# A three-part reordering in a Strassen-tiled flow-matching layer: the late half of pair 0, the first weight splits, and the last raw loads

## The chip, the cores and the metric

The kernel runs on one core of one Trainium2 chip. The metric is device time of one execution in microseconds (us). One core has TensorE (PE, matrix products into PSUM), VectorE (DVE), ScalarE (ACT), GpSimd (POOL), SyncE (SP, which here issues most DMAs) and 16 DMA engines. Each engine works through its own queue of instructions in order.

## The reference

One layer (`DEPTH = 1`) of a flow-matching backbone on 1024 sample tokens and 128 prompt tokens, `D_MODEL = 1024`, all in float32. For each group of tokens:

```python
h = rmsnorm(x, norm1_g) * (1.0 + scale1) + shift1
z = h @ w_in
# u_s5, u_f, g_s5, g_f are slices of z
y_s5, finals = s5_branch(u_s5, h0, p)        # two scans over a state space, GLU
y_f = fourier_branch(u_f)                    # 2D FFT, real part
m = sigmoid(g_s5) * (y_s5 @ w_proj_s5) + sigmoid(g_f) * (y_f @ w_proj_fft)
x = x + gate1 * (m @ w_out)
h2 = rmsnorm(x, norm2_g) * (1.0 + scale2) + shift2
ff = (silu(h2 @ w_ffn_gate) * (h2 @ w_ffn_up)) @ w_ffn_down     # D_FF = 2816
x = x + gate2 * ff
y = rmsnorm(x, final_norm_g)
```

The outputs are y of both groups and the final scan states of the prompt. The change works in the line of `ff`: the gate and up products and the down projection.

## The kernel before

All products are made in a split form: an operand is written as a high part (a cast to the `fp32r` type, on ACT) and a low part (operand minus high part, on DVE or POOL), and PE makes three products of the parts. So each weight block costs one cast and one subtraction, called a split here, before PE can use it.

**Feed-forward stage.** The 2816 hidden columns are 22 tiles of 128, taken as 11 pairs (`p` = 0 to 10). `ffn_unit(p, kind, which)` makes the gate (`"g"`) or up (`"u"`) half of a pair. It uses a Strassen-Winograd scheme: from the two weight tiles `w0` and `w1` four blocks `a11`, `a12`, `a21`, `a22` are taken, three sums and one more are formed on POOL, seven blocks are split, and seven products are made, in PSUM banks Z, W, X, Y, Z, X, Y. `which` says for which tokens: `"A"` is token tiles 0 to 4, `"B"` is token tiles 5 to 8, `"AB"` is both. The operands of B (`TB`) are written while the first unit already runs. So pair 0 runs in two halves: the early half `ffn_unit(0, ..., "A")` first, and the late half `ffn_unit(0, ..., "B")` after pair 2 in the kernel before. For the late half the splits are on DVE (function `le`), for the AB units on POOL.

The weights come through a ring of three buffers `ws`, with one exception: the gate weights of the late half (name `g0B`) go into the tile `gb` of the pool `pgb`, which is one buffer. The same buffer holds, one after the other, the gate rows `gb2`, the copy `hb` of token tile 6 in the first unit, and then `ra{m}`, the finished hidden rows of pair `m`, read back from the DRAM tensor `ffd` by `ra_load(m)`.

While pair `p` runs, the side work `a_steps(p - 1)` combines `ra` of the pair before in DVE sums, splits the results into `stg` (cast on ACT, subtraction on DVE) and writes them to the DRAM tensor `ad`: these are the Strassen operands of the down projection. It is hooked between the products of the units; pair 1 has no side work, and pair 0's is done under pair 10.

**Down stage.** The pairs are grouped in blocks: `BLK = [[0], [1, 2], [3, 4], [5, 6], [7, 8]]`, and `STD = [9, 10]`, which is made without Strassen. `prep(m, ki)` forms the weight block for product key `ki` (sums on POOL, or DVE for pairs 1 and 2), loads the activation operand A from `ad` (`load_at`) and splits the weight block (`split2`: cast on ACT, subtraction on POOL for pair 0, on DVE otherwise). The A operands of a block use a ring of 10 buffers; a block of two pairs has 14. The first block's sums go into ACC by copies on ACT (L1465), all others by additions on DVE (L1467). The seventh weight block of pair 0 takes a buffer `ftA` that the last unit of the feed-forward stage still uses.

For `STD`, `load_a(m)` reads the raw hidden rows `fr` from `ffd` and `prep_std` splits them on POOL; `gate_x` multiplies the sums by gate2 (DVE) and adds x1 (POOL), which `x1_load` reads into the ring `fr` (six buffers with the raw rows) or, one time in four, into `xr` (two buffers). At the end come the norm and the stores.

What sets the order: a planner simulates the engines and puts every instruction into its engine's queue as soon as, in its model, its operands and buffers are ready; where several are ready, the one earlier in the program goes first. So a load whose buffer is free can be queued far ahead of its place in the program. `tc.issue_after(ins)` holds a block's instructions behind `ins` on the same queue: in `load_a` and `x1_load`, behind `last["A"]`, and in the up units behind the last `ra_load`. No wait is added by it.

Of the kernel before, what the change touches and what calls it, by code (L numbers as in the profile page):

```python
# [61 lines left out]
def tile_flow_step(ctx: ExitStack, tc: tile.TileContext, a, o):  # L62
    nc = tc.nc
    V, S, PL, PE, SY = nc.vector, nc.scalar, nc.gpsimd, nc.tensor, nc.sync
# [23 lines left out]
    def f32(ap):  # L88
        return ap.bitcast(F32)
# [38 lines left out]
    mods, last = {}, {}  # L128
# [558 lines left out]
    def prep(q):  # L687
        return s5_prep2(q, *s5_prep(q))

    pre, run_ = [prep(0)], []  # L690
    gate(ORD[0])
    pre.append(prep(1))
    run_.append(s5_run(0, pre[0][1]))
    for q in range(NB):
        if q < NB - 1:
            run_.append(s5_run(q + 1, pre[q + 1][1]))
        if q:
            gate(ORD[q])
        if q == NB - 1:
            for p in ORD[NB:]:  # L700
                gate(p)
        s5_out(q, pre[q][0], pre[q][2], *run_[q])
        if q < NB - 2:
            pre.append(prep(q + 2))
# [416 lines left out]
    BLK = [[0]] + [[m, m + 1] for m in range(1, 9, 2)]  # L1121
    STD = [9, 10]

    def ra_load(m):
        ra[m] = pgb.tile([128, 2, NS], F32, tag="gb", name=f"ra{m}")
        for f in range(2):
            i_ = SY.dma_start(out=ra[m][:, f], in_=ffd[2 * m + f][:, 0:NS]).ins
        ra_ins[:] = [i_]

    def ffn_unit(p, kind, which, hooks=()):  # L1130
# [90 lines left out]
        if not gate_:  # L1221
            for s in which:
                _, nt, c0 = subs[s]
                st_ = dict(out=ffd[2 * p:2 * p + 2, :, c0:c0 + 128 * nt].rearrange("f p c -> p f c"),
                           in_=fsl[s].rearrange("p f t e c -> p f (t e c)"))
                if p == NF // 2 - 1:
                    last_st.append(st_)
                else:
                    SY.dma_start(**st_)
            if len(which) == 2 and p < STD[0] and p != 2:  # L1230
                ra_load(p)

    ps1 = open_pool("psF1", space=PSUM)
# [39 lines left out]
    def take(n, h=None):  # L1273
# [7 lines left out]
        return go  # L1281

    ffn_unit(0, "g", "A", [take(1), take(1), take(0), take(0), take(0, hk[0]), take(1, hk[1]), take(1, hk[2])])
    ffn_unit(0, "u", "A", [take(1, hk[3]), take(1), take(2, hk[4]), take(1, hk[5]), take(0), take(1), take(0)])
    pst_.release()
    ps2 = open_pool("psF2", space=PSUM)
    open_sub("B", {z: ps2 for z in "ZWXY"}, pm0, "m0a")
    ad = {m: dram.tile([7, 128, 2, 512], F32, tag=f"ad{m}", name=f"ad{m}") for m in range(STD[0])}
# [3 lines left out]
    def a_steps(m):  # L1292
        a_ = {f"{f}{z}": ra[m][:, f, h] for f in range(2) for z, h in (("L", LO), ("H", HI))}

        def comb(out, x, y, op=ALU.subtract):
            V.tensor_tensor(a_[out], a_[x], a_[y], op)  # L1296

        def p6():
            comb("0H", "0H", "1H", ALU.add)
            comb("0L", "0H", "0L")  # L1300

        def one(ki):
            nonlocal nstg
            src = a_[dict(P1="0L", P2="1L", P6="0L", P7="0L", P4="1H", P5="0H", P3="1L")[KEYS[ki]]]
            st_ = stg[:, nstg % 3]
            nstg += 1
            S.copy(out=st_[:, 0], in_=src)  # L1307
            V.tensor_tensor(st_[:, 1], src, f32(st_[:, 0]), ALU.subtract)  # L1308
            if m or ki not in (2, 3, 4):
                S.dma_start(out=ad[m][ki], in_=f32(st_))  # L1310

        def do(*fs):
            return lambda: [one(f) if isinstance(f, int) else f() for f in fs]

        p7a, p7b = (lambda: comb("1L", "1L", "0L")), (lambda: comb("0L", "1H", "0L"))
        st = [do(0), do(1), do(5), p6, do(p7a, 6), do(2), do(3), do(p7b, 4)]
        return [no] * 6 + st if m else [no] * 3 + st + [no] * 3

    for p in range(1, NF // 2):
        hk = a_steps((p - 1) % STD[0]) if p > 1 else [no] * 14  # L1320
        ffn_unit(p, "g", "AB", hk[:7])
        ffn_unit(p, "u", "AB", hk[7:])
        if p == 2:
            ffn_unit(0, "g", "B")
            ffn_unit(0, "u", "B")
            ra_load(2)
        if p == NF // 2 - 2:
            ra_load(0)

# [13 lines left out]
    AT, BT, PT, raws, araw, wraw = {}, {}, {}, {}, {}, {}  # L1343
# [12 lines left out]
    def a_new(name):  # L1356
        return pA.tile([128, 2, 512], F32R, tag="A", bufs=NA, name=name)

    def b_new(name):
        return ringed("b", [128, 2, 512], F32R, "wh", NWH, "R", NR, name)  # L1360

    def split2(w, src, eng=None):
        S.copy(out=w[:, 0], in_=src)
        (eng or V).tensor_tensor(w[:, 1], src, f32(w[:, 0]), ALU.subtract)  # L1364
        return w

    def load_at(m, ki):
        key = KEYS[ki]
        if (m, key) in AT:
            return  # L1370
        if m == 0 and ki in kept:
            AT[m, key] = kept[ki]
            return
        AT[m, key] = A1[:, ki] if m == 0 and ki < 2 else a_new(f"A{m}_{ki}")
        last["A"] = SY.dma_start(out=f32(AT[m, key]), in_=ad[m][ki]).ins

    def load_a(m):
        araw[m] = []
# [34 lines left out]
    def sub(out, x, y, op=ALU.subtract, eng=None):  # L1413
        (eng or PL).tensor_tensor(out, x, y, op)  # L1414

    def prep(m, ki):
        key = KEYS[ki]
        w0L, w0H, w1L, w1H = raws[m]
        if key == "P6":
            sub(w0H, w1H, w0H, eng=V if m in VSUB else PL)  # L1420
            sub(w0L, w0H, w0L, ALU.add, V if m in VSUB else PL)
        if key == "P5":
            sub(w1L, w1L, w0L)
            sub(w0L, w1H, w0L)
        bsrc = dict(P1=w0L, P2=w1L, P6=w0L, P7=w0H, P4=w1L, P5=w0L, P3=w1H)[key]
        if m == 0:
            B = wr.tile([128, 2, 512], F32R, tag="wh" if ki < 6 else "ftA", bufs=NWH if ki < 6 else 1, name=f"B0{key}")
        else:
            B = b_new(f"B{m}{key}")
        load_at(m, ki)  # L1430
        BT[m, key] = split2(B, bsrc, PL if m == 0 else V)

    def prep_std(m, ki):
        w0L, w0H, w1L, w1H = raws[m][0:4]
# [229 lines left out]
    for ki in range(2):  # L1664
        for m in BLK[1]:
            load_at(m, ki)
# [124 lines left out]
```

## Time and profile before

| | |
|---|---|
| three timed runs | 1547.5, 1546.07, 1540.08 us; median 1546.07 |
| the profiled execution | 1545.5 us, span 1543.5 us |
| mean granted clock of PE | 0.976 of full speed |
| PE busy | 1466.8 us, 95% of the span, 8999 matmuls |
| DVE, POOL, ACT busy | 61%, 43%, 37% of the span |
| DMA | 243.84 MB, mean 158 GB/s |

Times in the profile are microseconds from the start of the span; the span is the profiled execution without what lies around it. A busy share is an average over stages. An idle time is written in brackets with what ended it. PE's clock is given as the share of full speed that was granted: 1.00 is 2.4 GHz, and 0.5 is the lower level, 1.2 GHz. The feed-forward stage begins at about 745 us and ends at 1263 us; the down stage lasts from there to the end.

### The profile page before, as it was taken

How to read it: one execution, taken by the hardware profiler on the slowest of the kernel's cores; microseconds unless marked ns; L12 is line 12 of the kernel's file. 1: busy time of each engine (PE TensorE's matmuls, PEld its weight loads, DVE VectorE, ACT ScalarE, POOL GpSimd, SP SyncE). 2: the span in 40 equal slices, each digit the busy share in tenths (PEclk: the TensorE clock that was granted, in tenths of full speed). 3: DMA queues.
4: the chain of work that ended last, by engine and by line, in shares of the span. 5: the costliest groups of instructions: out<-in, count | busy, mean ns of one | idle time of the engine just before them, and what ended most of it. 6: DMA issues, size and time to landing. Idle time of an engine off the chain costs nothing. (4 is left out here: it accounts for less than half of the span.)

```text
span 1543.5 us, 23975 instructions
## 1 busy us (share of the span) xinstructions
PE 1466.8 (95%) x8999; PEld 1316.9 (85%) x8999; DVE 938.4 (61%) x1838; ACT 567.0 (37%) x1096; POOL 663.4 (43%) x606
## 2 busy tenths in 40 slices
PE   6999999999999999989999799999999999999995
PEld 3899998899968778877689799999999988888774
DVE  5647989995264335379942445554345547666778
ACT  7423334343543122255542233433333434212223
POOL 4900000000132111355687478877777982231354
PEclk9999999999989999999999899999999999999998
DMA  9242233232526643454513425444445557565713
GB/s 327 100 138 88 81 107 113 80 104 93 173 65 205 202 145 110 150 205 164 191 59 113 181 96 199 158 183 162 173 168 209 207 206 285 206 232 203 260 57 123
DMA packets 101984, 243.84 MB, mean 158 GB/s; under 512 B 15710, under 2 KB 46047, under 8 KB 101868
## 3 DMA queue, kind: packets, MB, share of 16 engines
q1 hardware_dynamic: 93228, 210.84, 39.9%
q10 hardware_dynamic: 8640, 31.46, 5.2%
q8 instruction: 71, 1.16, 0.3%
q14 instruction: 45, 0.37, 0.1%
HBM read 172.51 MB, written 69.74 MB: 157 GB/s over the span
## 5 line engine op out<-in xcount | busy, mean ns | idle before, releaser
L94 POOL TENSOR_TENSOR wh_glu<-ws_glu,wh_glu 128x512 fp32r<-128x512 f32 x4 | 5.1, 1278 | 338.0 <-ACT wh_glu L93 338.0
L271 PE MATMUL g<-h,wh_g 128*128 128x384 f32 (+1 forms) x432 | 147.3, 341 | 0.0
L272 PE MATMUL g<-h,wh_g 128*128 128x384 f32 (+1 forms) x432 | 147.1, 341 | 0.0
L273 PE MATMUL g<-h,wh_g 128*128 128x384 f32 (+1 forms) x432 | 146.3, 339 | 0.0
L1308 DVE TENSOR_TENSOR stg<-ra,stg 128x512 fp32r<-128x512 f32 x63 | 69.4, 1112 | 72.2 <-ACT stg L1307 72.0
L1414 POOL TENSOR_TENSOR wd<-wd,wd 128x512 f32<-128x512 f32 x25 | 36.7, 1481 | 110.6 <-DMA wd<-in_w_d 38.3
L272 PEld LDWEIGHTS g<-h,wh_g 128*128 128x128 f32 x432 | 81.4, 188 | 0.2 <-issue 0.2
L271 PEld LDWEIGHTS g<-h,wh_g 128*128 128x128 f32 x432 | 81.2, 188 | 0.3 <-issue 0.3
L273 PEld LDWEIGHTS g<-h,wh_g 128*128 128x128 f32 x432 | 81.2, 188 | 0.2 <-issue 0.2
L94 POOL TENSOR_TENSOR wh_pj<-ws_pj,wh_pj 128x512 fp32r<-128x512 f32 x16 | 22.1, 1382 | 103.9 <-ACT wh_pj L93 93.4
L1467 DVE TENSOR_TENSOR acc<-acc,U 128x1024 f32<-128x1024 f32 x34 | 41.4, 1219 | 26.8 <-PE U L1448 26.6
L1307 ACT CAST stg<-ra 128x512 fp32r<-128x512 f32 x63 | 38.3, 617 | 44.7 <-DVE ra L1296 32.2
L963 DVE TENSOR_TENSOR wh_out<-ws_out,wh_out 128x512 fp32r<-128x512 f32 x32 | 33.8, 1071 | 24.6 <-ACT wh_out L962 24.6
L1448 PE MATMUL q<-B,A 128*128 128x512 f32 x192 | 45.7, 394 | 0.5 <-DVE acc L1467 0.3
L1448 PEld LDWEIGHTS q<-B,A 128*128 128x128 f32 x192 | 35.8, 187 | 9.5 <-DVE acc L1467 0.8
L1296 DVE TENSOR_TENSOR ra<-ra 128x512 f32<-128x512 f32 x36 | 43.5, 1209 | 0.3
L963 POOL TENSOR_TENSOR wh_out<-ws_out,wh_out 128x512 fp32r<-128x512 f32 x16 | 22.4, 1405 | 48.8 <-ACT wh_out L962 45.7
L923 DVE TENSOR_TENSOR sgc<-sgc,p 128x384 f32<-128x384 f32 x24 | 13.3, 554 | 48.4 <-PE p L106 48.4
L977 PE MATMUL o<-wh_out,m 128*128 128x512 f32 x96 | 37.1, 414 | 4.1 <-ACT scr0b L1059 4.1
L636 DVE TENSOR_TENSOR ta<-X,Sg 128x56 f32<-128x56 f32 (+10 forms) x88 | 39.1, 445 | 1.2
L639 DVE TENSOR_TENSOR X<-X,tb 128x56 f32<-128x56 f32 (+10 forms) x88 | 39.1, 452 | 0.9
L962 ACT CAST wh_out<-ws_out 128x512 fp32r<-128x512 f32 x48 | 28.3, 615 | 30.4 <-PE o L979 20.3
(1550 smaller groups left out, 4522.3 us busy)
## 6 DMA issues: line engine op xcount, KB each, us to landing
ad<-stg ACTq DMA_DIRECT2D x60, 512.0 KB, 2.8
A<-ad SPq DMA_DIRECT2D x60, 512.0 KB, 5.8
wa<-in_w_ada SPq DMA_DIRECT2D x48, 512.0 KB, 6.0
ws_out<-in_w_out SPq DMA_DIRECT2D x24, 512.0 KB, 4.0
wd<-in_w_d SPq DMA_DIRECT2D x22, 512.0 KB, 9.1
ind<-in SPq DMA_DIRECT2D x54, 192.0 KB, 1.9
ws_g<-in_w_in SPq DMA_DIRECT2D x18, 512.0 KB, 3.5
sgc<-ind SPq DMA_DIRECT2D x48, 192.0 KB, 3.6
```

Of the source, the lines that this page charges most:

```text
L271: PE.matmul(ps, w[:, 0, wsl], hi, start=first, stop=False)
L272: PE.matmul(ps, w[:, 0, wsl], lo, start=False, stop=False)
L273: PE.matmul(ps, w[:, 1, wsl], hi, start=False, stop=last)
L636: V.tensor_tensor(A, src, Sc[:, 0, lv, gs].unsqueeze(1).unsqueeze(3).to_broadcast(shp), ALU.mult)
L639: V.tensor_tensor(dst, dst, B[:, ::-1], ALU.add)
L963: (eng or PL).tensor_tensor(w[:, 1, :], src, f32(w[:, 0, :]), ALU.subtract)
L977: PE.matmul(p, mc[t][0][:, k, ts_], w[n][:, 0], start=(k == 0), stop=False)
L1296: V.tensor_tensor(a_[out], a_[x], a_[y], op)
L1307: S.copy(out=st_[:, 0], in_=src)
L1308: V.tensor_tensor(st_[:, 1], src, f32(st_[:, 0]), ALU.subtract)
L1448: PE.matmul(ps, A[:, va], B[:, vb], start=(first and ti == 0 and i == 0), stop=(last and ti == n - 1 and i == 2), skip_group_check=True)
L1467: V.tensor_tensor(dst, dst, ps, ALU.add)
```

## The change

The late half of pair 0 moves from behind pair 2 to behind pair 1. With it `ra_load(1)` moves behind the late half, and `ra_load(2)` follows pair 2 as for the later pairs. The weight splits of pair 0 in the down stage go from POOL to DVE. The raw loads of pairs 9 and 10, and the x1 loads, are held behind the last A load of block 5 and 6 in place of that of block 7 and 8.

```diff
@@ -1227,7 +1227,7 @@
                     last_st.append(st_)
                 else:
                     SY.dma_start(**st_)
-            if len(which) == 2 and p < STD[0] and p != 2:
+            if len(which) == 2 and 1 < p < STD[0]:
                 ra_load(p)
 
     ps1 = open_pool("psF1", space=PSUM)
@@ -1320,10 +1320,10 @@
         hk = a_steps((p - 1) % STD[0]) if p > 1 else [no] * 14
         ffn_unit(p, "g", "AB", hk[:7])
         ffn_unit(p, "u", "AB", hk[7:])
-        if p == 2:
+        if p == 1:
             ffn_unit(0, "g", "B")
             ffn_unit(0, "u", "B")
-            ra_load(2)
+            ra_load(1)
         if p == NF // 2 - 2:
             ra_load(0)
 
@@ -1372,7 +1372,9 @@
             AT[m, key] = kept[ki]
             return
         AT[m, key] = A1[:, ki] if m == 0 and ki < 2 else a_new(f"A{m}_{ki}")
-        last["A"] = SY.dma_start(out=f32(AT[m, key]), in_=ad[m][ki]).ins
+        i_ = SY.dma_start(out=f32(AT[m, key]), in_=ad[m][ki]).ins
+        if m <= BLK[-2][-1]:
+            last["A"] = i_
 
     def load_a(m):
         araw[m] = []
@@ -1428,7 +1430,7 @@
         else:
             B = b_new(f"B{m}{key}")
         load_at(m, ki)
-        BT[m, key] = split2(B, bsrc, PL if m == 0 else V)
+        BT[m, key] = split2(B, bsrc, V)
 
     def prep_std(m, ki):
         w0L, w0H, w1L, w1H = raws[m][0:4]
```

## Rows read from the trace of the kernel before

**Rows 1.** two stretches of 100 us: busy us, instructions; clock, DMA share, GB/s.

```profile
800.00:900.00 100.00, 90.80 (x666) 90.01 (x665) 38.21 (x68) 32.58 (x67) 60.72 (x51) 0.93 0.34 124
1200.00:1300.00 100.00, 96.04 (x612) 89.35 (x613) 56.40 (x78) 41.11 (x75) 70.14 (x55) 0.98 0.67 245
```

**Rows 2.** waits of PE: who, for whom, us, times, longest.

```profile
PE ZBg0B L1162 <- ACT wh_g0Ba L962: 5.5, 1, 5.5
```

**Rows 3.** timeline of PE: start us, us, operation, count, [idle before <- releaser].

```profile
871.24 1.56 PE L1162 MATMUL YBu2AB<-TB,wh_u2ABs 128*128 128x256 f32 x12
878.32 3.29 PE L1162 MATMUL ZBg0B<-TB,wh_g0Ba 128*128 128x256 f32 x12 [5.52 <-ACT wh_g0Ba L962]
...
892.33 1.58 PE L1162 MATMUL ZBg0B<-TB,wh_g0Ba 128*128 128x256 f32 x12
...
906.46 1.92 PE L1162 MATMUL ZAg3AB<-TA,wh_g3ABa 128*128 128x320 f32 x12
```

**Rows 4.** timeline of the SP queue around the late half of pair 0.

```profile
872.56 0.33 SPq L1138 DMA_DIRECT2D ws_g0B<-in_w_g  x1
...
900.01 0.33 SPq L957 DMA_DIRECT2D ws_g3AB<-in_w_g  x1
```

**Rows 5.** timeline of POOL: last reader of the buffer that g0B loads into.

```profile
763.09 1.28 POOL L1076 TENSOR_TENSOR TB<-hb,TB 128x512 fp32r<-128x512 f32 x1 [2.14 <-ACT TB L1074]
```

**Rows 6.** line 963, the splits: ns min/median/max, first and last start.

```profile
L963 DVE TENSOR_TENSOR wh_u0Ba<-ws_u0B,wh_u0Ba x3: 680/686/1742, 892.3 to 898.2; 128x512 fp32r<-128x512 f32 x3
```

**Rows 7.** one stretch of the late half, columns as in Rows 1.

```profile
892.00:906.50 14.50, 14.50 (x126) 14.50 (x125) 9.19 (x17) 5.64 (x12) 6.80 (x6) 1.00 0.42 146
```

**Rows 8.** the first 14 us of the down stage, columns as in Rows 1.

```profile
1263.50:1277.50 14.00, 10.35 (x39) 7.97 (x38) 2.78 (x3) 5.12 (x7) 10.92 (x11) 0.88 0.98 352
```

**Rows 9.** timeline of all engines where the down stage begins.

```profile
1263.54 2.97 PE L1448 MATMUL U<-B0P,A 128*128 128x512 f32 x12
...
1271.38 0.62 ACT L1363 CAST B0P<-wd 128x512 fp32r<-128x512 f32 x1 [3.16 <-POOL fsA L1190]
1271.90 1.92 ACT L1465 COPY acc<-U 128x1024 f32<-128x1024 f32 x2
...
1272.96 2.50 PE L1448 MATMUL U<-B0P,stg 128*128 128x512 f32 x6 [3.65 <-ACT acc L1465]
```

**Rows 10.** line 1364, splits of the down stage: ns min/median/max.

```profile
L1364 POOL TENSOR_TENSOR B0P<-wd,B0P x7: 1252/1292/1743, 1256.8 to 1273.2; 128x512 fp32r<-128x512 f32 x7
L1364 DVE TENSOR_TENSOR B1P<-wd,B1P x7: 680/685/1219, 1284.3 to 1320.5; 128x512 fp32r<-128x512 f32 x7
```

**Rows 11.** the SP queue in the last two blocks of the down stage.

```profile
1393.78 9.57 SPq L1375 DMA_DIRECT2D A<-ad  x3
...
1407.87 20.38 SPq L1375 DMA_DIRECT2D A<-ad  x10
...
1447.85 1.37 SPq L1382 DMA_DIRECT2D fr<-ffd  x3
```

**Rows 12.** timeline of POOL, first splits of the last pairs' activations.

```profile
1454.61 1.40 POOL L1364 TENSOR_TENSOR A<-fr,A 128x512 fp32r<-128x512 f32 x1 [23.00 <-DMA fr<-ffd]
```

**Rows 13.** timeline of DVE in the same place.

```profile
1457.61 3.48 DVE L1364 TENSOR_TENSOR B<-wd,B 128x512 fp32r<-128x512 f32 x2
```

**Rows 14.** timeline of PE in the same place.

```profile
1465.74 1.65 PE L1448 MATMUL V<-B7P,A 128*128 128x512 f32 x3 [2.50 <-DVE acc L1467]
...
1468.47 1.48 PE L1448 MATMUL V<-B7P,A 128*128 128x512 f32 x3
```

**Rows 15.** that stretch as a whole, columns as in Rows 1.

```profile
1461.00:1478.40 17.40, 14.20 (x49) 10.41 (x48) 12.97 (x10) 4.99 (x9) 9.90 (x7) 0.80 0.52 173
```

**Rows 16.** timeline of PE, first products of the last full block.

```profile
1416.66 0.86 PE L1448 MATMUL U<-B7P,A 128*128 128x512 f32 x3
...
1419.46 0.85 PE L1448 MATMUL Y<-B7P,A 128*128 128x512 f32 x3
```

**Rows 17.** DMA issues, 1400 to 1420 us: count, KB, us to landing.

```profile
A<-ad SPq DMA_DIRECT2D x8, 512.0 KB, 4.8
```

## Prediction

> **What bounds the kernel now.** I read the busy time by stretches of 100 us first. TensorE (PE) is the bound: in the down stage and in the feed-forward stage it is busy nearly all the time, so only the stretches where it falls short can pay. Two of them lie where the change works [rows 1]: 90.8 of 100 us at 800 to 900, and 96.0 at 1200 to 1300. A third, at 1461 to 1478, shows in a narrower cut [rows 15]. The table of PE's waits then names who ends each gap; the largest in the touched code is one of 5.5 us for the first split weight of the late gate unit, g0B [rows 2]. The timelines of PE, of SP's queue and of POOL tell why each gap is there. Outside these stretches PE runs through, so a gap that closes moves all later work forward, as long as DMA and VectorE (DVE) can follow.
>
> **Part 1: the late half behind pair 1.** The last product of pair 2 starts at 871.24, and pair 3 starts at 906.46 [rows 3]. A late product has 12 matmuls; ten of them run from 892.33 to 906.46, so one takes 1.41 us. Pair 2 therefore ends at 872.65, and 33.8 us pass for 14 late products that need 14 x 1.41 = 19.8 us: 14.0 us are lost, in gaps and at a lower clock behind them. The cause stands in SP's queue: the load of g0B's weights is issued only at 872.56 [rows 4], when pair 2 is over, because it goes into the one buffer `gb`, which then holds ra1, the input of the side work of pair 2. With the change, nothing is loaded into that buffer before the late half: its previous reader, the split of `hb`, is over at 764.4 [rows 5], long before pair 1 ends. The load can then lie under the early half and pair 1. The step takes all its instructions along: on SP the two loads into `gb`, u0B's two weight loads and one store, and behind them ra1's two loads, which pass from the end of pair 1 to the end of the late half; ra2's two no longer wait for the late half. ra1's sums and splits stay under pair 2, in the second half of their hooks, and as many as before.
>
> What could be late next: the seven splits of each late unit are on DVE. Uncontended one takes 0.69 us, at worst 1.74 [rows 6]. While u0B ran at full pace, DVE was busy 9.2 of 14.5 us with splits and sums together [rows 7], so it has 5.3 us in 14.5 to spare. Pair 2's second gate weight needs a slot that u0B's splits free. Before, the same load for pair 3 went out at 900.01, 6.5 us before pair 3, and PE did not wait for it [rows 3, 4]. So the gain is bounded by 14.0 above, and by nothing below if these covers fail. I take 13.5, near the upper end, since u0B already ran without a gap on the same engines.
>
> Here the Trainium skill speaks against the move (page "SBUF — State Buffer", section "Who interferes with whom"): a VectorE instruction with two SBUF inputs and a GpSimd instruction that reads SBUF block one another for a whole instruction. The trace agrees in that the same split takes 0.69 or 1.74 us.
>
> **Part 2: first weight splits on DVE.** The down stage begins at 1263.54, makes 36 matmuls' worth of work and stops: the next product waits 3.65 us, until 1272.96, for ACT's copy of U out of PSUM [rows 9]. That copy was ready long before, but on ACT it is queued behind a cast at 1271.38, which waits for POOL's last product of the feed-forward stage (fsA). POOL is late because seven splits of 1.29 us each, 9.0 us, stand among its work [rows 10]; it is busy 10.9 of 14.0 us [rows 8]. On DVE the same split takes 0.69 us (B1's row), 4.8 us in all, and DVE is busy only 2.8 of these 14.0 us [rows 8, 10]; at the worst of that row, 1.22 us, 8.5 us would still fit. The stretch holds 39 matmuls; one costs 0.233 us at the full clock (12 from 1416.66 to 1419.46 [rows 16]), so 9.1 of 14.0 us are work and 4.9 are lost. That is the upper bound. The lower is 0: the 16 DMA engines are busy 0.98 of this stretch at 352 GB/s [rows 8], with the first block's operands and the next weights in the same queue, and PE running ahead of them would wait there. Between, I take 4.0, nearer the upper end, because the first products have their operands and the wait named is not a DMA.
>
> **Part 3: raw loads one block ahead.** The four raw loads of pairs 9 and 10 (fr) and the x1 loads of the end are held behind the last A load. They go out at 1447.85 [rows 11], and POOL's first A split has waited 23.0 us for them [rows 12]. Then POOL's eight A splits, DVE's eight weight splits and the gate products crowd together: two DVE splits take 3.48 us [rows 13], the sum out of V comes late, and PE waits 2.5 us and then runs on the lower of its clock levels (six matmuls from 1465.74 to 1468.47, 0.455 us each) [rows 14]. From 1461.0 to 1478.4 there are 49 matmuls, 11.4 us of work in 17.4 [rows 15]: 6.0 us lost, the most that this part can return.
>
> It has a price. The loads now follow the last A load of pair 6, issued by 1403.35, and go ahead of pair 7's first, issued at 1407.87 [rows 11]. Eight loads have a buffer at once: four raw ones, two x1 in the same ring of six, two in the ring `xr`. Each is 512 KB; at 352 GB/s (0.524 MB in 1.49 us) they are 11.9 us of DMA. Pair 7's first A load lands 4.8 us after its issue [rows 17], at 1412.7, and is used at 1416.66 [rows 16]: 4.0 us of slack. If the eight stand ahead in one queue, 4.5 us of their 11.9 are over by 1407.87 and 7.4 come on top, so PE waits 3.4 us, and about 12 matmuls at the lower clock add 12 x 0.222 = 2.7. That is a loss of 6.1 against a gain of at most 6.0. If they slip between, the 6.0 stand. I take a net gain of 1.0, near the middle, nearer the loss, since A loads wait for buffers and SP will find the others ready first.
>
> A rule of the Trainium skill leans the same way (page "DMA: Bandwidth & Descriptors", section "Queues, rings and completion order"): each DMA engine takes descriptors of a queue in ring order. No run here shows the order of two such loads; by the rule the 6.1 us loss would come in full and the sum would be 1.0 smaller.
>
> **Sum.** 13.5 + 4.0 + 1.0 = 18.5 us off the profiled execution's own 1545.5, which is 0.6 under the median of the runs: 1527.0 us. DVE's chain at the very end follows PE and moves with it. Half a per cent, 7.7 us, is about what a measurement of this kernel can tell from no change.
>
> **Rivals.**
> 1. All three parts pay in full: 14.0 + 4.9 + 6.0 = 24.9, so 1520.6. For it: each gap has a named cause that the diff takes away. Against: the full DMA at 1263 and the queue order at 1403. 0.22.
> 2. Only the late half pays, with DMA taking part 2 and the early loads taking part 3: 13.5, so 1532. For it: the 0.98 DMA share. 0.17.
> 3. DVE becomes the bound in the late half, by the blocking of DVE and POOL: if all 14 splits take 1.74 instead of 0.69, DVE has 14.7 us more to do; in 19.8 us it has 7.2 to spare, so 7.5 us come back as PE's wait and part 1 shrinks to 6. With 4 and 1 that is 11, so 1534.5. For it: POOL now prepares pair 2 at the same time. Against: only some splits of u0B were slow. 0.08. The rule from the Trainium skill's page "SBUF — State Buffer", above, is this mechanism.
> 4. The change does not do what it says: the wait moves from g0B's load to pair 2's second gate weight, whose slot u0B frees late, and costs the same 14.0. Parts 2 and 3 leave 5, so 1540.5, no change that can be told. Against: the 6.5 us of lead before pair 3. 0.08.
> 5. Slower: in block 7 and 8 the moved loads stay ahead of pair after pair of A loads, and PE works at the lower clock through the block. Its 192 matmuls would lose 0.222 each, 43 us. It outweighs the other parts' 17.5 from 79 matmuls on, and makes the kernel measurably slower (25.2 us) from 114 on; at a whole block the time is 1571. For it: eight loads are two thirds of a block's 14 A loads in bytes. Against: between 1416 and 1460 PE leaves DMA time to catch up, and one delay should be all. 0.05.
>
> **How the numbers follow.** My forecast has 0.40; rivals 1 to 5 have 0.22, 0.17, 0.08, 0.08 and 0.05. The time is the forecast's, 1527. Its own range is 1522 to 1531. The range for 8 in 10 takes in rivals 1 to 3, with some 4 us around them for what a newly ordered schedule does elsewhere: 1517 to 1539. Faster by over half a per cent holds the forecast and rivals 1 to 3, 0.87; within it rival 4, 0.08; slower rival 5, 0.05.
>
> **What would show it.** Right: g0B's loads issued before pair 1 begins, no PE gap between pair 1 and pair 2, 14 late products in about 20 us at the full clock; B0 splits on DVE near 0.7 us, U's copies at about 1267 less the 14 us already gained, no wait of PE for ACT there; raw loads out some 25 us before block 7 and 8 ends, no 2.5 us wait for the sum of V. Wrong: a PE wait for a DMA of A at the start of block 7 and 8, for weights of pair 2, or for a late split in u0B; DMA ending the idle time behind the first products of the down stage. A tail behind PE that grows by what PE saves would break the assumption that the end moves with PE.

## The result, and the profile after

The changed kernel takes 1526.66 us (median of four runs, 1526.42 to 1527.39), against 1546.78 for the kernel before in the same series. The ratio is 0.9879, 95% interval 0.985 to 0.9908: 1.2% faster, some 18.7 us (the two medians lie 20.1 us apart; the kernel before ran between 1540.08 and 1548.13). The profiled execution's span is 1524.6 us against 1543.5; PE is busy 1460.6 us of it, 96%, at a mean clock of 0.981.

To see where the time came from, the span is cut at first products on PE's timeline. Each row is the difference of two starts in one profile.

| stretch | before | after | gain |
|---|---|---|---|
| start of the span to pair 1's up unit | 806.08 | 808.84 | -2.8 |
| from there to pair 3 (that unit, pair 2, late half) | 100.38 | 86.18 | 14.2 |
| pair 3 to the down stage | 357.08 | 356.67 | 0.4 |
| the down stage's first U product to its first V product | 13.87 | 12.20 | 1.7 |
| from there to the first block's end | 11.05 | 11.06 | 0.0 |
| blocks 1/2 to 7/8, up to the first Zp product of 7/8 | 187.08 | 181.85 | 5.2 |
| from there to the end | 67.96 | 67.80 | 0.2 |

The sum is 18.9 us, the difference of the spans.

The changed kernel by stretches, with the columns of [rows 1]; the first two are the stretches shown there, the others are used further down.

```profile
800.00:900.00 100.00, 100.00 (x778) 100.00 (x777) 45.27 (x75) 38.08 (x77) 79.98 (x66) 1.00 0.33 119
1200.00:1300.00 100.00, 98.03 (x587) 88.92 (x586) 69.59 (x91) 40.04 (x70) 58.47 (x44) 0.98 0.70 253
1389.00:1410.00 21.00, 19.69 (x85) 15.73 (x85) 13.97 (x13) 3.69 (x7) 6.32 (x4) 1.00 0.95 360
1400.00:1500.00 100.00, 98.69 (x429) 80.11 (x428) 79.29 (x83) 26.92 (x56) 45.50 (x26) 1.00 0.42 157
```

PE is busy for all of 800 to 900, where it had 90.8, and for 98.0 of 1200 to 1300, where it had 96.0.

PE's timeline where the late half now runs, answering to [rows 3]:

```profile
829.62 1.56 PE L1162 MATMUL YBu1AB<-TB,wh_u1ABs 128*128 128x256 f32 x12
831.02 1.56 PE L1162 MATMUL ZBg0B<-TB,wh_g0Ba 128*128 128x256 f32 x12
...
850.62 1.93 PE L1162 MATMUL ZAg2AB<-TA,wh_g2ABa 128*128 128x320 f32 x12
```

The last product of pair 1 starts at 829.62, the first late one 1.40 us behind it, and pair 2 follows at 850.62. So 14 late products take 19.6 us, 1.40 each; before, 33.8 us passed there. The SP queue, answering to [rows 4]:

```profile
768.54 0.33 SPq L1138 DMA_DIRECT2D ws_g0B<-in_w_g  x1
...
799.05 13.66 SPq L957 DMA_DIRECT2D ws_u0B<-in_w_u  x2
...
838.70 0.81 SPq L1127 DMA_DIRECT2D ra<-ffd  x2
843.65 0.33 SPq L957 DMA_DIRECT2D ws_g2AB<-in_w_g  x1
```

g0B's load goes out at 768.54, 62 us before its first product; it was issued after pair 2's end before. ra1 takes the same buffer from 838.70. Pair 2's second gate weight goes out at 843.65, 7.0 us before pair 2.

DVE's splits of the late half, by form (instructions | busy us, mean ns | idle before):

```profile
L963 DVE TENSOR_TENSOR wh_u0Ba<-ws_u0B,wh_u0Ba 128x512 fp32r<-128x512 f32 x3 | 3.0, 990 | 0.2
L963 DVE TENSOR_TENSOR wh_g0Ba<-ws_g0B,wh_g0Ba 128x512 fp32r<-128x512 f32 x2 | 2.3, 1158 | 0.5 <-ACT wh_g0Ba L962 0.5
L963 DVE TENSOR_TENSOR wh_u0Bs<-ws_u0B,wh_u0Bs 128x512 fp32r<-128x512 f32 x3 | 2.0, 690 | 1.3 <-ACT wh_u0Bs L962 1.1
```

Their means are 0.69 to 1.16 us, between the two ends of [rows 6], and no product waits for one. The timelines tell when a split is slow. Of this trace's 155 DVE splits of this shape from the feed-forward stage on, 74 began while POOL was idle, and none of these took over 0.70 us; 81 began while a POOL instruction was running, and 70 of these took over 0.8 us.

All engines where the down stage begins, answering to [rows 9]; in brackets, the idle time and what ended it:

```profile
1250.22 1.30 POOL L1416 TENSOR_TENSOR wd<-wd,wd 128x512 f32<-128x512 f32 x1
...
1251.56 1.67 ACT L1363 CAST B0P<-wd 128x512 fp32r<-128x512 f32 x3 [4.32 <-POOL wd L1416]
...
1252.21 0.69 DVE L1364 TENSOR_TENSOR B0P<-wd,B0P 128x512 fp32r<-128x512 f32 x1 [2.65 <-ACT B0P L1363]
...
1253.38 0.86 POOL L1190 TENSOR_TENSOR fsA<-fsA,ftA 128x320 f32<-128x320 f32 x1 [1.86 <-DVE ftA L1172]
1253.55 1.23 DVE L1364 TENSOR_TENSOR B0P<-wd,B0P 128x512 fp32r<-128x512 f32 x1
...
1254.71 0.47 DVE L1172 TENSOR_TENSOR ftA<-ftA,YAu10AB 128x320 f32<-128x320 f32 x1
...
1255.24 2.20 PE L1450 MATMUL U<-B0P,A 128*128 128x512 f32 x6 [1.98 <-DVE ftA L1172]
...
1256.23 0.62 ACT L1363 CAST B0P<-wd 128x512 fp32r<-128x512 f32 x1 [3.01 <-POOL fsA L1190]
1256.76 1.92 ACT L1467 COPY acc<-U 128x1024 f32<-128x1024 f32 x2
...
1261.09 2.96 PE L1450 MATMUL U<-B0P,stg 128*128 128x512 f32 x12
```

The old wait for ACT's copy of U is gone, and another stands in its place. After six matmuls PE waits 1.98 us for a DVE sum into ftA (1254.71). The last sums of the feed-forward stage are queued on DVE behind a weight split (1252.21) that has waited 2.65 us for ACT's cast (1251.56), which waits for POOL's weight sum (1250.22). A second split stands ahead of that sum too (1253.55); beside POOL's fsA (1253.38) it takes 1.23 us. The copy of U (1256.76) still stands behind a cast that waits for POOL's fsA, as before.

The seven splits as a group, answering to [rows 10]:

```profile
L1364 DVE TENSOR_TENSOR B0P<-wd,B0P 128x512 fp32r<-128x512 f32 x7 | 8.2, 1166 | 2.8 <-ACT B0P L1363 2.6
```

They cost DVE 8.2 us, 1.17 each, nearer to the POOL figure of [rows 10] (1.29) than to the 0.69 that I had taken from DVE's. The two that began with POOL idle took 0.68 and 0.69 us, the five beside a POOL instruction 1.01 to 1.78.

Near the end, PE, answering to [rows 14, 16]:

```profile
1404.60 0.97 PE L1450 MATMUL V<-B5P,A 128*128 128x512 f32 x3 [1.31 <-DVE acc L1469]
...
1410.26 0.86 PE L1450 MATMUL U<-B7P,A 128*128 128x512 f32 x3
...
1449.63 0.85 PE L1450 MATMUL V<-B7P,A 128*128 128x512 f32 x3
...
1456.80 0.85 PE L1450 MATMUL Zp<-B7P,P 128*128 128x512 f32 x3
```

SP's queue there, answering to [rows 11]:

```profile
1389.87 1.48 SPq L1384 DMA_DIRECT2D fr<-ffd  x3
...
1393.80 2.42 SPq L1544 DMA_DIRECT2D x<-x1d  x2
...
1398.46 1.58 SPq L1375 DMA_DIRECT2D A<-ad  x2
```

DMA issues from 1397 to 1412, answering to [rows 17]:

```profile
A<-ad SPq DMA_DIRECT2D x10, 512.0 KB, 10.2
```

And POOL's first activation splits, answering to [rows 12]:

```profile
1438.10 6.93 POOL L1364 TENSOR_TENSOR A<-fr,A 128x512 fp32r<-128x512 f32 x4 [22.80 <-ACT A L1363]
```

The raw loads go out at 1389.87 and the x1 loads from 1393.80, ahead of pair 7's first A load at 1398.46. By the semaphore updates in the trace, the loads from 1389.87 on land one after another in the order of their issue, about 1.3 us apart: the first raw load at 1397.11, this A load at 1408.77. That is 10.3 us after its issue, where the same load took 4.0 in the kernel before (1407.87 to 1411.90). Its product, U<-B7P, starts at 1410.26 without a wait, 1.5 us behind the landing; the only new wait is 1.31 us for a DVE sum at 1404.60. V at 1449.63 does not wait, where 2.5 us and a lower clock stood in [rows 14]. POOL now waits for ACT's cast of the A operand, not for the DMA.

### The profile page after: what moved, and what is told of

Read it like the earlier page. It is cut to its first block, busy times and chain, and to the rows that moved or that the text cites. A ratio compares the mean times of both kernels' runs of the same rounds, so it can differ in the third digit from the quotient of the medians.

```text
span 1524.6 us, 23986 instructions
## 1 busy us (share of the span) xinstructions
PE 1460.6 (96%) x8999; PEld 1312.5 (86%) x8999; DVE 946.5 (62%) x1845; ACT 567.1 (37%) x1096; POOL 662.1 (43%) x599
## 3 DMA queue, kind: packets, MB, share of 16 engines
q8 instruction: 71, 1.16, 0.3%
## 5 line engine op out<-in xcount | busy, mean ns | idle before, releaser
L962 ACT CAST wh_out<-ws_out 128x512 fp32r<-128x512 f32 x48 | 28.2, 616 | 29.2 <-PE o L979 18.9
```

## The experiments

The three parts alone first: each is the kernel before with one part of the diff. `e1_late` has the first two hunks, `e2_split` the last line, `e3_loads` the hunk on `last["A"]`.

> Only the late half of pair 0 is moved behind pair 1; splits and raw loads are as in the kernel before. Theory A (the single buffer gb was the whole cause of the gap, and nothing behind it takes the time back): 14 us less than before, about 1532, with no PE wait between pair 1 and pair 2. Rival B (part of it is given back, since the down stage or the end is paced by something that does not move with PE): under 11 us less, above 1535, and the stretch from the first product of the down stage to the last product grows by the difference.

> Only the weight splits of pair 0 in the down stage are on DVE. Theory A (the difference of the two traces: a new wait behind a DVE sum takes 2 us of what the old wait behind ACT gives back): 1.5 to 2 us less than before, hardly to be told from no change, and a PE wait of about 2 us ended by DVE among the first products. Rival B (forecast): 4 us less, with no wait of PE there over 0.5 us.

> Only the raw and x1 loads are held behind the last A load of block 5 and 6. Theory A (the moved loads slip between the A loads, and PE at the end is no longer held up by sums that stand behind crowded splits): 4.5 to 5.5 us less than before; the wait of 2.5 us for the sum of V near 1465 is gone, and PE's clock stays full there. Rival B (forecast): about 1 us less, since pair 7's first A load comes 3 us late and PE waits for a DMA at about 1417.

| part alone | ratio, 95% interval | median | its own stretch, before -> here |
|---|---|---|---|
| late half | 0.9934, 0.9915 to 0.9952 | 1534.16 | 100.38 -> 86.19 |
| splits on DVE | 0.9984, 0.9968 to 1.0 | 1540.75 | 13.87 -> 12.84 |
| early loads | 0.9981, 0.9963 to 0.9999 | 1541.03 | 187.08 -> 181.84 |

The stretch of the late half gains 14.2 us, as in the full change, though the timed gain is 10.2 us (7.4 to 13.1): in this profile the part of the kernel ahead of it took 809.78 us, where that of the kernel before took 806.08. To see whether that is chance, the same kernel was run again.

> The late half alone once more, with more rounds. In its first profile the stages from pair 1 to the end took 15.1 us less than before, but the runs only 10.2 (7.4 to 13.1). Theory A (the part in front, where the order of all queues is the same, came out 3.7 us longer by chance): 13 to 15 us less this time. Rival B (it is longer in this kernel in every execution): again about 10 us less, and the first up product of pair 1 again at about 810 us.

It gave 0.9912 (0.9888 to 0.9935), 13.6 us, and its profile has 86.19 in the stretch and again 809.87 ahead of it: the time is what theory A expected, the front part what rival B did, so the question stays open. Over the 14 profiles of this study that front part lasts from 804.98 to 813.69 us, and the feed-forward stage's first product, ahead of everything that any of these kernels changes, starts between 734.36 and 740.13. I did not find what sets it; for one part of the change a stretch between two products tells more than the total.

The splits alone gain 1.0 us in their stretch, with the same new wait as in the full change, a little longer. PE's timeline of that kernel:

```profile
1260.18 1.57 PE L1448 MATMUL U<-B0P,A 128*128 128x512 f32 x6
1264.38 2.84 PE L1448 MATMUL U<-B0P,A 128*128 128x512 f32 x6 [2.62 <-DVE ftA L1172]
```

The early loads alone gain their 5.2 us in full in their stretch; the timed runs show 2.9 us (0.2 to 5.7), with 809.41 us ahead of pair 1's up unit in the profile. Of the splits alone the timed runs tell nothing (an interval up to 1.0).

**Is it the buffer or the place?** The late half stays behind pair 2, but its gate weights come through the ring `ws` like all others (kernel before):

```diff
-        if nm == "g0B":
-            gbw = pgb.tile([128, 2048], F32, tag="gb", name="ws_" + nm)
...
-        else:
-            w0 = weight_ws(src[2 * p], nm + "0")
...
+        w0 = weight_ws(src[2 * p], nm + "0")
```

> The late half stays behind pair 2, but its gate weights go through the ring ws as all others do, not into the buffer gb. Theory A (the buffer is the cause, the place is not): the gap of 14 us behind pair 2 goes nearly as in the changed kernel, 11 to 14 us less than before. Rival B (the place matters, since behind pair 2 the ring's slots and the late half's splits on DVE meet the side work of pair 1): 8 us less or worse, with PE waiting in g0B for weights or splits.

Ratio 0.9958 (0.9943 to 0.9974), 1538.47 us: 6.5 us (4.0 to 8.8) by the timed runs, which is rival B's band. The stretch takes 91.49: 8.9 of the 14.2 us are gained, between the two bands. PE's timeline of it:

```profile
870.42 1.56 PE L1156 MATMUL YBu2AB<-TB,wh_u2ABs 128*128 128x256 f32 x12
871.82 1.56 PE L1156 MATMUL ZBg0B<-TB,wh_g0Ba 128*128 128x256 f32 x12
...
887.16 0.79 PE L1156 MATMUL WBu0B<-TB,wh_u0Bs 128*128 128x256 f32 x2 [3.61 <-ACT wh_u0Bs L962]
```

And its SP queue:

```profile
855.81 0.33 SPq L957 DMA_DIRECT2D ws_u0B<-in_w_u  x1
...
876.42 1.20 SPq L957 DMA_DIRECT2D ws_u0B<-in_w_u  x1
```

The gate half now runs behind pair 2 without a gap (871.82). But u0B's second weight is issued only at 876.42, when a slot of the three-buffer ring comes free, and behind a store that waited 16.9 us for POOL's fsA in the same queue. PE waits 3.61 us for its split at 887.16, and the clock is 0.72 from there to 896.75. So the buffer `gb` was the cause of the old 5.52 us wait, as the forecast had it. The 5.3 us that stay come with this late load. Behind pair 1, `gb` is free as well and u0B's two loads go out 32 us and 19 us before the late half begins (799.05 and 812.38, against 831.02). Whether the place itself costs anything is not shown: no run has the late half behind pair 1 with its gate weights in the ring.

**Where is the rest of part 2?** Three edits of the changed kernel shift the load between DVE, POOL and ACT. `e5_subs` also puts pair 0's four weight sums on DVE, `e6_mix` puts the splits of the last weight blocks back on POOL, and `e10_copy` is `e6_mix` with the first two copies of U on DVE instead of ACT:

```diff
 e5_subs (VSUB: the pairs whose other two sums are on DVE)
-VSUB = (1, 2)
+VSUB = (0, 1, 2)
...
-            sub(w1L, w1L, w0L)
-            sub(w0L, w1H, w0L)
+            sub(w1L, w1L, w0L, eng=V if m == 0 else PL)
+            sub(w0L, w1H, w0L, eng=V if m == 0 else PL)
 e6_mix
-        BT[m, key] = split2(B, bsrc, V)
+        BT[m, key] = split2(B, bsrc, PL if m == 0 and ki > 2 else V)
 e10_copy, besides
-            add_to(cc(0, 0, r), U[r], first)
+            if first:
+                V.tensor_copy(cc(0, 0, r), U[r])
+            else:
+                add_to(cc(0, 0, r), U[r])
```

> The changed kernel, with the four sums of pair 0's weight blocks (before the products P6 and P5) on DVE too, 0.69 us each there, so that nothing of pair 0's preparation is left on POOL. Theory A (the new wait of 2.0 us arises because DVE's fifth split waits for a cast that waits for POOL's sums, and the last sums of the feed-forward stage stand behind it on DVE): the wait goes, the stretch from the first product of the down stage to the first V product falls from 12.2 to about 9.5 us, and the time by 2 to 3 us against the changed kernel. Rival B (the DMA queue, busy 0.98 of this stretch before, holds PE there): the stretch stays at 11 us or more, with a wait ended by DMA. Rival C (DVE is now too long a queue): a longer wait for a DVE sum.

> The changed kernel, with the last four of pair 0's seven splits back on POOL and the first three on DVE. Theory A (what DVE's queue suffers from is the splits that depend on POOL's second pair of sums; the first three are harmless): the wait for the DVE sum is gone, the wait for ACT behind POOL comes back in part; the stretch takes 10.5 to 13 us against 12.2 in the changed kernel. Rival B (any split left on POOL makes the last products of the feed-forward stage as late as before): 13.5 us or more.

> The variant with three splits of pair 0 on DVE and four on POOL, and in addition the first two copies of U out of PSUM on DVE, which is free there, in place of ACT. Theory A (what is left of the wait at the begin of the down stage is ACT's queue alone: the copies stand behind the cast into ftA): no PE wait among the first products, the stretch from the first product to the first V product falls from 10.1 to 8.4 to 8.9 us, and the time by 1 to 1.5 us, to about 22 us under before. Rival B (DMA or POOL's splits hold PE next): the stretch stays at 10 us with another name on the wait.

| kernel | ratio, 95% interval | median | U to V | pair 1's up unit to the first Zp of 7/8 |
|---|---|---|---|---|
| after | 0.9879, 0.985 to 0.9908 | 1526.66 | 12.20 | 648.0 |
| after, run again | 0.9878, 0.9847 to 0.9909 | 1525.89 | 12.49 | 646.6 |
| e5_subs | 0.9865, 0.9827 to 0.9903 | 1524.15 | 9.77 | 647.3 |
| e6_mix | 0.9864, 0.9831 to 0.9897 | 1523.47 | 10.13 | 645.2 |
| e10_copy | 0.9859, 0.9837 to 0.9881 | 1522.75 | 8.41 | 643.4 |

> The changed kernel once more, beside the three variants on the same chip: 20 us less than before, the same waits as in its first profile. What stands in front of the feed-forward stage, where both programs have the same order, may differ by some 3 us from one execution to the next, as it did between the first two profiles.

The second run of the changed kernel shows what a profile repeats to: 646.6 against 648.0 us in the last column. In `e5_subs` the U to V stretch is 2.4 us shorter than after, as its theory A has it, but the wait for DVE is halved and not gone, and PE now also waits ahead of the stretch: 0.75 us for a DVE sum in the last unit and, for its first product, 0.64 us for an A load. PE's waits in this place:

```profile
PE U L1450 <- DVE ftA L1172: 1.0, 1, 1.0
PE XAu10AB L1162 <- DVE ftA L1172: 0.8, 1, 0.8
PE U L1450 <- DMA A<-ad: 0.6, 1, 0.6
```

In `e6_mix` the wait for ftA is gone and the old one for ACT's copy comes back at a smaller size:

```profile
1256.75 3.07 PE L1450 MATMUL U<-B0P,stg 128*128 128x512 f32 x12 [1.46 <-ACT acc L1467]
```

With that copy on DVE as well, the waits of PE from 1200 to 1275 are an empty list: 8.41 us for 36 matmuls of 0.233 us, 8.4. This is the whole of what the stretch can give, 5.5 us under before. So DMA did not bound it: from the first U product on, the 16 DMA engines are 0.98 busy for 14 us in the changed kernel and 0.93 in `e10_copy`, at 342 GB/s in both. The order in the queues of DVE and ACT did. By its median `e10_copy` is the fastest kernel run here (by its ratio 21.8 us under before), but its interval overlaps that of the change; in its profile the part ahead of pair 1's up unit took 813.69 us, the longest of all.

**Is part 2 needed in the combination?** The change without its last line, splits on POOL:

> The changed kernel without its second part: all splits of pair 0 on POOL as before. Theory A (the parts add up, and the second is worth what its stretch shows): the stretch from the first product of the down stage to the first V product goes back from 12.3 to 13.9 us or a little more, and the time is 1.5 to 2.5 us above the changed kernel. Rival B (the splits on DVE also delay the end of the feed-forward stage, by what they take from its sums): the stages before gain as much as this one loses, no difference in the sum.

Ratio 0.9866 (0.9839 to 0.9892), 1523.7 us, and U to V takes 9.31: less than with part 2. In blocks 1/2 to 7/8, further on, this kernel takes 183.28 us where the changed kernel takes 181.85, so part of this is lost again. PE's and POOL's timelines of it:

```profile
1253.85 3.06 PE L1450 MATMUL U<-B0P,stg 128*128 128x512 f32 x12 [0.65 <-ACT acc L1467]
```

```profile
1237.63 1.73 POOL L1364 TENSOR_TENSOR B0P<-wd,B0P 128x512 fp32r<-128x512 f32 x1
```

And the same place in the late half alone, run again, which has the same splits on POOL:

```profile
1262.98 4.47 PE L1448 MATMUL U<-B0P,stg 128*128 128x512 f32 x12 [5.24 <-ACT acc L1465]
```

```profile
1246.81 1.75 POOL L1364 TENSOR_TENSOR B0P<-wd,B0P 128x512 fp32r<-128x512 f32 x1
```

The same wait for ACT's copy is 0.65 us in one and 5.24 in the other. Two profiles of the late half alone have 14.55 and 15.31 for the stretch. In `e9_nosplit` POOL begins the splits of this stage 9.8 us before PE ends the feed-forward stage (1247.43), in the late half run again 5.2 us before (1251.97). All six profiles with these splits on POOL give one rule. From the first split on POOL's order is the same in them, without a pause, and the copy of U starts 15.1 to 15.2 us behind POOL's first split. So this lead and the wait always add up to 10.4 us:

| kernel | POOL's lead | PE's wait | sum |
|---|---|---|---|
| e9_nosplit | 9.80 | 0.65 | 10.45 |
| e1_late | 6.94 | 3.50 | 10.44 |
| e4_late_ws | 6.87 | 3.57 | 10.44 |
| e3_loads | 6.81 | 3.62 | 10.43 |
| before | 6.77 | 3.65 | 10.42 |
| e1_again | 5.15 | 5.24 | 10.39 |

The size of the wait that part 2 aims at is thus set by when POOL's chain of work begins. It begins with a weight sum that a load of `wd` releases, 12.8 us before the down stage in `e9_nosplit`, 8.1 in the late half run again and 9.6 to 9.9 in the others. Why it comes so early in `e9_nosplit` stays open, with one profile of that kernel. In `e10_copy` the same sum begins 8.9 us before the down stage, so its missing wait is no such luck. What is shown: the stretch can be short with the splits on POOL, and in the timed runs it makes no difference that can be told (0.9866 and 0.9879 with overlapping intervals).

**What does part 3 gain, and where?** `e7_raw_only` is the change with the x1 loads held as before behind the last A load of block 7 and 8; `e8_two` holds raw and x1 loads one block earlier still:

```diff
 e7_raw_only
+        last["all"] = i_
...
-        with tc.issue_after(last["A"]):
+        with tc.issue_after(last["all"]):
 e8_two
-        if m <= BLK[-2][-1]:
+        if m <= BLK[-3][-1]:
```

> The changed kernel, with only the four raw loads ahead and the x1 loads behind the last A load of block 7 and 8, as before. Theory A (the raw loads alone give the 5 us at the end): the stretch from the first product of block 1 to the last sums of block 7 and 8 stays within 0.5 us of the changed kernel's 181.9 us, and half of the DMA load ahead of pair 7 is gone, so the new wait of 1.3 us near 1403 goes if DMA had a part in it. Rival B (the early x1 loads matter, since they let POOL's additions of the end start sooner): the stretch behind it, to the end, grows by 1 us or more over 67.8.

> The changed kernel with the raw and x1 loads held behind the last A load of block 3 and 4, two blocks ahead in place of one. Theory A (one block ahead is early enough, POOL's A splits now wait for free A buffers): within 1 us of the changed kernel from block 1 to the end, if the planner finds an order without a wait again; the rows to look at are PE waits ended by a DMA near block 5 and 6. Rival B (the crowding of DMA is only moved to another block and costs more there): 2 us or more slower.

| kernel | ratio, 95% interval | median | blocks 1/2 to 7/8 | behind |
|---|---|---|---|---|
| e7_raw_only | 0.9901, 0.9863 to 0.994 | 1529.91 | 184.76 | 67.94 |
| e8_two | 0.9916, 0.9895 to 0.9936 | 1531.93 | 187.14 | 68.88 |

Their intervals overlap that of the change, so it is the stretches that tell them apart. For `e7_raw_only` neither expectation came out: the blocks lose 2.9 us of the gain, and the stretch behind does not grow.

In `e7_raw_only` PE's queue keeps pair 7's first product early, among block 5 and 6's V products, and it waits for its A load:

```profile
1406.36 0.94 PE L1451 MATMUL U<-B7P,A 128*128 128x512 f32 x3 [1.23 <-DMA A<-ad]
```

This is the price that the forecast set at 3.4 us and a lower clock, at 1.23 us: the load goes out at 1396.19 and lands at 1406.23, behind four raw loads and two of `wd`, and the clock stays at 1.00 behind the wait. The wait of V for DVE is back too, 1.59 us, though the raw loads went out at 1391.71, as early as in the change. In `e8_two` they go out at 1346.74, and the whole gain is gone:

```profile
1451.79 0.94 PE L1450 MATMUL q<-B,A 128*128 128x512 f32 x3 [1.05 <-DVE acc L1469]
1454.35 1.07 PE L1450 MATMUL V<-B7P,A 128*128 128x512 f32 x3 [1.61 <-DVE acc L1469]
...
1456.49 1.49 PE L1450 MATMUL V<-B7P,A 128*128 128x512 f32 x3
```

PE waits for DVE's sums, and groups of three matmuls behind take up to 1.49 us in place of 0.84: the lower clock again, a mean of 0.79 from 1452 to 1460. DVE's timeline shows where it differs. In `e8_two` the sum that q waits for (1450.44) stands behind two weight splits and a gate2 product:

```profile
1446.48 2.90 DVE L1364 TENSOR_TENSOR B<-wd,B 128x512 fp32r<-128x512 f32 x2
1449.30 1.21 DVE L1550 TENSOR_TENSOR acc<-acc,g5s 128x1024 f32<-128x1024 f32 x1
1450.44 1.21 DVE L1469 TENSOR_TENSOR acc<-acc,V 128x1024 f32<-128x1024 f32 x1
```

The changed kernel in the same place:

```profile
1442.10 4.08 DVE L1364 TENSOR_TENSOR B<-wd,B 128x512 fp32r<-128x512 f32 x3
...
1450.86 1.23 DVE L1550 TENSOR_TENSOR acc<-acc,g5s 128x1024 f32<-128x1024 f32 x1
```

In the change the splits are over at 1446.18, four sums follow one another from 1446.10 to 1449.61, and the next gate2 product comes behind them, at 1450.86. So the raw data's arrival alone does not decide; with the data early, the wait still comes back when DVE's splits and gate2 products are queued ahead of the sums. That the order on DVE is the whole cause was not tried by itself.

## Why the prediction was right, and where its steps were not

**The total** came out at 1526.66 where 1527.0 was forecast, and the profile's gain from pair 1 on is 21.7 us where the sum said 18.5; 2.8 us were lost ahead of pair 1's up unit, all of them before the feed-forward stage begins (its first product starts at 737.41, before at 734.42). So much of the agreement is luck: the terms of parts 2 and 3 were mis-sized in opposite directions, by 2.3 and 4.2 us, and the loss in front, which no part of the sum covers, took back most of what was left.

**Part 1, 13.5 forecast, 14.2 measured.** Each step held: the load issued before pair 1, no gap on either side, 1.40 us per late product at full clock. The bound of 14.0 was passed by 0.2 mostly since 14 products also ran at 1.40 instead of 1.41 us each. Rival 4, the wait that moves to pair 2's second gate weight, fell: that load was 7.0 us ahead. Rival 3, DVE as the bound, fell: from 831 to 850.6 DVE was busy 11.28 and POOL 10.93 of 19.6 us. Splits beside a POOL instruction did take longer, so the two engines do interfere; it was not enough to matter in this part. The direction agrees with the rule of the Trainium skill's page "SBUF — State Buffer", section "Who interferes with whom".

**Part 2, 4.0 forecast, 1.7 and 1.4 measured (1.0 alone).** The mis-sized term is "the first products have their operands": the splits became DVE work that waits, through ACT's cast, for POOL's weight sums, which stayed on POOL, and the last sums of the feed-forward stage stood behind them in DVE's queue. I had counted DVE's busy share (2.8 of 14 us) and not what is queued behind a waiting instruction. The splits were also 1.17 us instead of 0.69, since five of the seven ran beside POOL. Two readings were off as well. The stop comes after 24 matmuls and not 36; the whole stretch from U to V holds 36, or 8.4 us, so 5.5 us were lost in it and not 4.9. And the seven splits alone do not make POOL late: with the same splits on POOL, `e9_nosplit` waits 0.65 us, since POOL began earlier. The lower bound, DMA, was not the reason: `e10_copy` removes the whole loss under the same DMA load.

**Part 3, 1.0 forecast, 5.2 measured.** The mis-sized term is the price of 6.1 us; the gain of up to 6.0 was about right. The step "PE waits 3.4 us" took PE's order as given, with U<-B7P at a fixed place. The planner built the order anew: in the change this product stands behind block 5 and 6's remaining products and starts 11.8 us after its load's issue, where it was 8.8 before ([rows 11, 16]). The other half of the step, that the loads stand ahead in one queue, held: DMA was 0.95 busy from 1389 to 1410, the loads landed in the order of their issue, and the A load took 10.3 us instead of 4.0. At the old distance of 8.8 us PE would have waited 1.5 us for it, by an estimate from these figures, and not 3.4; in `e7_raw_only`, where the order kept the product early, it waited 1.23. The landings agree with the rule of ring order (the Trainium skill, page "DMA: Bandwidth & Descriptors", section "Queues, rings and completion order"), but the full loss that I had worked out by it did not come. The prediction also says that no run shows the order of two such loads; the landing times of the change do show it. And the reason given for the gain, that the raw loads were late for POOL, was not enough: `e7_raw_only` and `e8_two` have them early and keep V's wait.

**The end** moved with PE, as assumed: 67.8 to 68.0 us behind the first Zp in every kernel but `e8_two` (68.88).

Rival 1 with 24.9 us was too high mainly by the part 2 term; for parts 1 and 3 it came nearer than the forecast. Rival 2 with 13.5 was too low, and rival 5's block at the lower clock did not appear: the clock of 1400 to 1500 was 1.00.

## What to carry to other kernels

A wait whose cause is a buffer shared with unrelated data could be forecast well here: the time to the buffer's last reader and the length of the gap gave the gain within a microsecond. When work moves to an engine with a low busy share, look instead at what its queue holds behind the moved instruction and at what that instruction itself waits for: here the splits took their wait along, and a free engine gained 1.7 us of a possible 5.5. Price an instruction by those of its kind that run beside the same neighbours, too: 0.69 us with POOL idle became 1.17 on average. And where a planner writes the order, an edit can reorder the products around it. A price that assumed the old order came out too high here (6.1 us, where PE waited for no such load), and the same edit taken one step further returned the whole gain.

## What was unexpected of the hardware

The same work does not take the same time: the part ahead of the feed-forward stage, which no kernel here changes, took between 734.36 and 740.13 us over 14 profiles, a spread of 5.8 us, about a third of what the change gains. The same DVE split of 128x512 took 0.67 to 0.70 us whenever it began with POOL idle, in all 14 profiles, and 1.3 us on average, up to 2.9, when a POOL instruction was running. And the loads of SP's queue landed in the order of their issue wherever I looked near the end of five profiles, so a load of 512 KB put behind seven others still under way came 10.3 us after its issue instead of 4.0.
